# End of both mixers: half of the output projection held behind the last paged steps, and fewer, spread sums of squares in the attention's norm

## The chip, the cores and the metric

The kernel runs on one core of a Trainium2 chip. The metric is the device time of one execution in microseconds (us), as the median of several runs. The engines are named as the profile names them: PE (TensorE matmul), PEld (TensorE weight load), DVE (VectorE), ACT (ScalarE), POOL (GpSimd), SP (SyncE, which here only starts DMAs). TensorE's clock has two levels, 1.2 and 2.4 GHz; the profile gives the granted clock as a share of the higher one.

## The reference

One inference step of a decoder trunk with two layers, on 592 tokens together: 16 meta tokens and 512 prompt tokens of one sequence, and 8 sequences of 8 new tokens each. A layer is a half-step SwiGLU FFN, a mixer, and a second half-step FFN, each behind an RMSNorm and each added to the stream `x`. The mixer:

```python
z, xbc, dt_raw, q, k, v = split(h @ lp['w_in'])
y_ssd = ...                      # conv, SSD scan, gate, grouped RMSNorm: 512 columns
o = sb_block(q, ..., k_all, v_all, ...)   # stick-breaking attention, 8 heads x 64
y_sb = rms_norm(o.reshape(b, L, SB_WIDTH), lp['sb_out_norm'])
out = jnp.concatenate([y_ssd, y_sb], axis=-1) @ lp['w_out']
x = x + out
```

The prompt attends to itself. Each of the 8 sample sequences attends to 2048 old tokens, whose keys and values lie in pages of a cache, and to its own 8 new ones. The norm of `y_sb` needs for each token the sum of squares of all 512 attention outputs.

## The kernel before, in words

The stream lies in eight tiles `x` of 128 channels by 592 tokens. Every large product is made of three float32r products of split operands (high x high, high x low, low x high): `mm3` (L597) issues them for two halves of the tokens, 296 columns each (288 in the second mixer), so a weight block of 512 x 128 costs 24 matmuls at L602. `gemm` (L630) takes two such blocks per call: it loads the raw weights by SP (L584), splits them on ACT (L593) and DVE (L594), runs `mm3`, and then calls a function `done` on the PSUM result.

The program is written in one order, and the tile framework's planner then fixes, before the launch, the order of the instructions on each engine; an engine runs its instructions in that fixed order. The planner takes, of the instructions that its own clock holds ready, the one with the lowest number. `ahead` (L617) gives numbers inside the mixer, from the tables `PRI` and `UNIT` (L96, L97). Of those that meet here, in order: `wo0` 0, `wo3` 86, `wo6` 529, `pw7` 619, `tail` 799, `pv7` 1019, `ps7` 1031, `wo4` 1087, `wo7` 1477, `wo5` 1599, `wo2` 1775, `wo1` 2358. The program is traced once; the numbers are the same in both kernels.

The paged attention (`past`, L1444) goes through the 8 sample sequences. For each, `past_scores` (`ps`) gathers the keys by indirect DMAs of POOL (L1473, buffers `kn`, 6 of them), transposes them on DVE into `kt` (L1479, 2 buffers), multiplies (`sc`, recorded at L208 and L211) and takes two sigmoids. `past_weights` (`pw`) does the running products, a carry over 4 segments (L1504 to L1512), and 8 transposes on PE (L1520) that ACT copies to `wt`. `past_values` (`pv`, L1527) gathers values into 8 tiles `v`, from the same 6 buffers `kn`, and multiplies them by `wt` into `po` in four groups; then a mask (`ob`, L1550), a small product (L1554) and a copy (L1555) put 8 columns into `oP`, which after the eighth sequence has all 64.

`w_out` has 1024 rows. Its first 512 belong to the SSD half, and their product (L772, MH and ML, units `wo0` to `wo7` of 24 matmuls, 192 in all) needs nothing of the attention; `odone` adds it to `x` (L769). Behind these gemms in the program, the sample part is finished: `oP` times `tn` plus `on` (L774, L775, whole), and copies into the attention tiles `OT` (shown as `q`, L777, L778). `mix_sb` (L1258) makes the split operands `mh`, `ml` of `OT` (L1267, L1268) and the squares `gsq` (L1271), four tiles each, and calls `factor` (L553). `factor` starts a flow: one step of it is taken at each matmul of `mm3` (`step`, L607). Its first number is how many steps it waits, its third how many between the sums and the spread of the result; the second was read by nothing. It multiplies the squares by a column of ones to get one sum per token (`token_sums`, L472: five groups of 128 tokens times as many tiles as there are; each such matmul stands as two instructions at L476), takes 1/sqrt on DVE (L522 to L529, 14 small instructions with L566), and spreads it over the partitions with ten matmuls (L538) into `R` (L571). The second 512 rows of `w_out` (L793, again 192 matmuls) run meanwhile; their `last` (L784) needs `R`: it multiplies, adds to `x` (L789) and makes the operands of the next FFN and its sums of squares (`norm_tile`, L440, with an addition on POOL at L459).

## Time and profile before

| | |
|---|---|
| time, median of 3 runs | 2736.54 us (2730.8 to 2743.09) |
| the profiled execution: its own time | 2746.03 us |
| its span / mean granted clock | 2744.0 us / 0.975 |
| PE busy in it | 2641.0 us (96%) |
| DVE, ACT, POOL busy | 1502.8, 976.7, 313.4 us |
| HBM | 124 GB/s over the span |

The mixer of the first layer ends at about 962 us of the span, that of the second at about 2322. The FFNs lie before, between and behind. In the views a row of a stretch gives the busy time of each engine in it, the granted clock and the share of DMA; a row of the timeline gives start, duration, engine, line, operation, what it writes and reads, and in brackets how long its engine had been idle before it and what ended that.

### The profile page before, as it was taken

What the parts mean: (1) busy time and instruction counts of PE and PEld (TensorE: products, weight loads), DVE (VectorE), ACT (ScalarE), POOL (GpSimd) and SP (SyncE); (2) the same over time, 40 slices, a digit from 0 to 9 for tenths busy, and PEclk for the clock granted to TensorE, in tenths of its full rate; (3) what the DMA queues carried; (4) which work ended last, traced back from release to release, by engine and by line L of the source; (5) the groups of instructions that cost most, each with busy time, mean ns of one, the idle gap of its engine ahead of it and who ended that gap; (6) DMA issues with size and microseconds to landing.
All of it is one profiled execution on the core that took longest, in us unless ns stands there. A gap on an engine that the chain in (4) does not pass through costs nothing. (4 is left out here: it accounts for less than half of the span.)

```text
span 2744.0 us, 51377 instructions
## 1 busy us (share of the span) xinstructions
PE 2641.0 (96%) x21587; PEld 2497.2 (91%) x21587; DVE 1502.8 (55%) x2993; ACT 976.7 (36%) x1769; POOL 313.4 (11%) x288
## 2 busy tenths in 40 slices
PE   8999999999888899999999999999998899999999
PEld 7999999888657899999999999998876579999999
DVE  5444346477876544443554343455788856444444
ACT  3323224355663332222332222233556533322222
POOL 1000000023442100000000000000334421000000
PEclk9999999999998899999999999999999998999999
DMA  3232234357875122222222223243568751222222
GB/s 110 78 115 85 82 103 128 125 160 262 281 251 194 54 85 78 77 85 83 73 85 77 93 86 100 73 155 124 193 234 282 266 173 55 85 78 92 78 85 82
DMA packets 245110, 343.27 MB, mean 125 GB/s; under 512 B 32808, under 2 KB 196720, under 8 KB 244880
## 3 DMA queue, kind: packets, MB, share of 16 engines
q1 hardware_dynamic: 208016, 205.77, 23.7%
q0 software_dynamic: 36864, 134.23, 14.2%
q8 instruction: 169, 2.77, 0.4%
q14 instruction: 61, 0.50, 0.1%
HBM read 320.29 MB, written 19.66 MB: 124 GB/s over the span
## 5 line engine op out<-in xcount | busy, mean ns | idle before, releaser
L602 PE MATMUL g<-xl,whi 128*128 128x296 f32 (+1 forms) x3392 | 1018.7, 301 | 0.9 <-DVE xl L447 0.9
L602 PE MATMUL g<-xh,wlo 128*128 128x296 f32 (+1 forms) x3392 | 1013.5, 300 | 3.4 <-DVE wlo L594 3.4
L602 PE MATMUL g<-xh,whi 128*128 128x296 f32 (+1 forms) x3392 | 1014.9, 300 | 1.6 <-DVE gs L231 1.2
L593 ACT ACTIVATE whi<-raw 128x512 fp32r<-128x512 f32 (+1 forms) x664 | 412.8, 622 | 1373.7 <-PE g L602 1309.5
L594 DVE TENSOR_TENSOR wlo<-raw,whi 128x512 fp32r<-128x512 f32 (+1 forms) x664 | 450.7, 679 | 596.2 <-ACT whi L593 543.2
L602 PEld LDWEIGHTS g<-xh,wlo 128*128 128x128 f32 x3392 | 641.4, 189 | 5.8 <-DVE wlo L594 4.1
L602 PEld LDWEIGHTS g<-xh,whi 128*128 128x128 f32 x3392 | 640.4, 189 | 6.6 <-issue 3.0
L602 PEld LDWEIGHTS g<-xl,whi 128*128 128x128 f32 x3392 | 641.7, 189 | 4.0 <-issue 2.2
L602 PE MATMUL g<-hl,whi 128*128 128x296 f32 (+1 forms) x1408 | 417.8, 297 | 0.0
L602 PE MATMUL g<-hh,wlo 128*128 128x296 f32 (+1 forms) x1408 | 417.7, 298 | 0.0
L602 PE MATMUL g<-hh,whi 128*128 128x296 f32 (+1 forms) x1408 | 416.7, 298 | 0.0
L1473 POOL DMA_INDIRECT kn<-in_cache_k,ki x128 | 142.5, 1113 | 1546.7 <-PE g L602 931.4
L602 PEld LDWEIGHTS g<-hl,whi 128*128 128x128 f32 x1408 | 265.2, 188 | 0.0
L602 PEld LDWEIGHTS g<-hh,wlo 128*128 128x128 f32 x1408 | 264.4, 188 | 0.0
L602 PEld LDWEIGHTS g<-hh,whi 128*128 128x128 f32 x1408 | 263.9, 188 | 0.0
L1479 DVE STREAM_TRANSPOSE kt<-kn 128x512 f32<-128x512 f32 x256 | 163.6, 680 | 30.6 <-DMA kn<-in_cache_k,ki 17.2
L1537 POOL DMA_INDIRECT v<-in_cache_v,vi x128 | 137.2, 1072 | 336.0 <-PE po L211 175.2
L698 DVE SCALAR_TENSOR_TENSOR x<-g,x 128x296 f32<-128x296 f32 (+1 forms) x192 | 88.2, 464 | 118.9 <-PE g L602 118.4
L231 DVE TENSOR_TENSOR us<-g,R 128x296 f32<-128x296 f32 (+1 forms) x176 | 81.6, 464 | 130.5 <-PE g L602 130.4
L231 DVE TENSOR_TENSOR gs<-g,R 128x296 f32<-128x296 f32 (+1 forms) x176 | 80.7, 464 | 124.3 <-PE g L602 121.3
L602 PE MATMUL g<-mh,whi 128*128 128x296 f32 (+1 forms) x256 | 83.0, 332 | 4.8 <-ACT mh L1267 4.6
L602 PE MATMUL g<-ml,whi 128*128 128x296 f32 (+1 forms) x256 | 85.1, 333 | 0.0
(372 smaller groups left out, 2910.9 us busy)
## 6 DMA issues: line engine op xcount, KB each, us to landing
raw<-in_ffn_w_gu SPq DMA_DIRECT2D x176, 512.0 KB
raw<-in_ffn_w_down SPq DMA_DIRECT2D x80, 512.0 KB
raw<-in_w_in SPq DMA_DIRECT2D x44, 512.0 KB
raw<-in_w_out SPq DMA_DIRECT2D x16, 512.0 KB
spill<-x SPq DMA_DIRECT2D x16, 296.0 KB
x<-spill SPq DMA_DIRECT2D x16, 296.0 KB
raw<-in_ffn_w_down SPq DMA_DIRECT2D x16, 256.0 KB
xt<-in_x_prompt SPq DMA_DIRECT2D x8, 256.0 KB
```

What stands on the lines that cost most here:

```text
L231: self.nc.vector.tensor_tensor(tv[0:P, h, :], ps[h][0:P, 0:self.n], rv[0:P, h, :], ALU.mult)
L593: nc.scalar.activation(hi[:, 0:nk], s, AF.Copy)
L594: nc.vector.tensor_tensor(lo[:, 0:nk], s, hi[:, 0:nk].bitcast(F32), ALU.subtract)
L602: nc.tensor.matmul(ps[h][:, 0:self.n], w[:, k, :], self.hv(x)[:, h, :], start=(first and k == 0 and i == 0), stop=(last and k == nk - 1 an ...
L698: nc.vector.scalar_tensor_tensor(v, p, 0.5, v, ALU.mult, ALU.add)
L1473: nc.gpsimd.indirect_dma_start(kn, None, self.kflat, bass.IndirectOffsetOnAxis(ap=self.kidx[l][:, s, i:i + 1], axis=0))
L1479: nc.vector.transpose(kt[:, 2 * u:2 * u + 2].rearrange("p t h i -> p t (h i)"), kns[u][:, :, 256 * quad:256 * quad + 256])
L1537: nc.gpsimd.indirect_dma_start(v.rearrange("p k c -> p (k c)"), None, self.vflat, bass.IndirectOffsetOnAxis(ap=self.vidx[l][:, i, e:e + 1] ...
```

## The change

Three edits at the end of the mixer, and one in a helper.

1. Every matmul of the units `wo0` to `wo7` gets a dependency of order alone (no semaphore) on an instruction of the last paged steps: `wo0` to `wo3` on the last score matmul, `wo4` and `wo5` on the last transpose of the weights, `wo6` and `wo7` on the last value matmul. The planner may place them on PE only behind it.
2. The last two value tiles of the eighth sequence use the two buffers `kt` (the same 4096 bytes per partition) in place of `kn`.
3. `oP` is finished in two column ranges, 0 to 56 and 56 to 64, and its last addition writes into `OT` itself; the copies at L778 go.
4. `mix_sb` makes all of `mh` and `ml` first, then the squares, and adds them in pairs on DVE, so that two tiles go to `token_sums`. `factor` now waits 8 steps before the sums and takes two steps from sum to sum. The other two users of `factor` give 0 as the second number, which means one step as before.

```diff
             P = B[:, 0:5].unsqueeze(2)
-            yield from self.token_sums(P, squares, self.c_ones)
+            for _ in self.token_sums(P, squares, self.c_ones):
+                for _ in range(wait[1] or 1):
+                    yield
...
-    def mm3(self, ps, hi, lo, nk, XH, XL, first, last):
+    def mm3(self, ps, hi, lo, nk, XH, XL, first, last, after=None):
...
+                    if after:
+                        self.tc.add_manual_dep(mm, after.name, mybir.DependencyInfo(
+                            mybir.DependencyClass.NoSync, mybir.DependencyReason.DATA), reason="behind")
                     self.step()
...
         for mp in range(4):
-            self.gemm(wo, 0, 4, mp * 256, MH, ML, lambda m, ps: odone(2 * mp + m, ps))
-        nc.vector.tensor_tensor(self.oP, self.oP, self.tn, ALU.mult)
-        nc.vector.tensor_tensor(self.oP, self.oP, self.on, ALU.add)
+
+            self.gemm(wo, 0, 4, mp * 256, MH, ML, lambda m, ps: odone(2 * mp + m, ps),
+                      after=(self.last_sc, self.last_sc, self.last_pw, self.last_po)[mp])
         for m in range(4):
             nc.vector.tensor_copy(OT[m][:, 512:528], self.tail[:, m, :])
-            nc.vector.tensor_copy(OT[m][:, 528:592], self.oP[:, m, :])
+        for a, b in ((0, 56), (56, 64)):
+            o = self.oP[:, :, a:b]
+            nc.vector.tensor_tensor(o, o, self.tn[:, :, a:b], ALU.mult)
+            for m in range(4):
+                nc.vector.tensor_tensor(OT[m][:, 528 + a:528 + b], o[:, m, :], self.on[:, m, a:b], ALU.add)
...
+        for m, t in enumerate(OT):
             s = self.tmp("gsq")
             nc.scalar.activation(s[:, a:b], t[:, a:b], AF.Square)
-            sq.append(s)
-        self.factor(sq, 1.0 / 512, (0, 8, 20))
+            if m % 2:
+                nc.vector.tensor_tensor(sq[-1][:, a:b], sq[-1][:, a:b], s[:, a:b], ALU.add)
+            else:
+                sq.append(s)
+        self.factor(sq, 1.0 / 512, (8, 2, 20))
...
-                    v = self.kv.tile([128, 2, 512], F32, name="v", tag="kn", bufs=6)
+                    tag, bufs = ("kt", 2) if s == 7 and e + a2 == 2 else ("kn", 6)
+                    v = self.kv.tile([128, 2, 512], F32, name="v", tag=tag, bufs=bufs)
```

`self.last_sc`, `self.last_pw` and `self.last_po` are set to each score matmul, weight transpose and value matmul as it is issued, so that they hold the last of the layer; `gemm` hands `after` on to `mm3`.

## Rows read from the trace of the kernel before

**Rows 1.** The page's first part: busy time of each engine, its share of the span, and its instructions.
```profile
PE 2641.0 (96%) x21587; PEld 2497.2 (91%) x21587; DVE 1502.8 (55%) x2993; ACT 976.7 (36%) x1769; POOL 313.4 (11%) x288
```

**Rows 2.** Stretches of 5 us around the end of the first mixer. Columns: the stretch, its length, busy us (and instructions) of PE, PEld, DVE, ACT, POOL, granted clock, DMA share, GB/s.
```profile
835.00:840.00 5.00, 4.53 (x52) 3.68 (x52) 5.00 (x13) 3.03 (x5) 1.66 (x2) 0.50 0.36 107
855.00:860.00 5.00, 5.00 (x46) 4.21 (x45) 1.90 (x4) 2.21 (x5) 0.00 (x0) 1.00 0.32 105
900.00:905.00 5.00, 0.41 (x11) 0.34 (x12) 0.00 (x0) 0.00 (x0) 0.61 (x1) 0.99 0.61 210
920.00:925.00 5.00, 5.00 (x23) 5.00 (x24) 1.08 (x7) 0.28 (x1) 0.00 (x0) 0.50 0.00 0
```

**Rows 3.** The instructions of L602 alone in four stretches, two of each mixer: the stretch, its length, PE's busy us (count), PEld's, the granted clock, DMA share, GB/s.
```profile
849.50:865.30 15.80, 13.66 (x91) 12.60 (x91) 1.00 0.29 97
910.00:931.00 21.00, 17.53 (x64) 14.45 (x64) 0.63 0.09 26
2210.00:2218.60 8.60, 3.44 (x22) 2.99 (x22) 1.00 0.67 207
2267.00:2291.00 24.00, 18.08 (x65) 14.78 (x66) 0.58 0.07 23
```

**Rows 4.** What PE waited for in 840 to 915 us, and what POOL waited for in 840 to 905: the engine, line and tile that waited, for what, us in total, times, the longest.
```profile
PE po L208 <- DMA v<-in_cache_v,vi: 4.6, 1, 4.6
PE g L602 <- ACT mh L1267: 2.3, 1, 2.3
POOL v L1537 <- PE po L211: 41.3, 5, 22.1
```

**Rows 5.** The same for PE in 2205 to 2270 us.
```profile
PE g L602 <- ACT mh L1267: 2.4, 1, 2.4
```

**Rows 6.** The timeline of all engines at the end of the first mixer's paged part.
```profile
898.16 1.20 POOL L1537 DMA_INDIRECT v<-in_cache_v,vi  x1 [16.20 <-PE po L211]
904.61 0.38 PE L208 MATMUL po<-v,wt 128*32 128x256 f32 x1 [4.59 <-DMA v<-in_cache_v,vi]
906.32 0.42 DVE L1550 TENSOR_TENSOR ob<-po,call 128x256 f32<-128x256 f32 x1 [7.77 <-PE po L211]
906.79 1.04 PE L1554 MATMUL po<-call,ob 128*128 128x16 f32 x4 [0.52 <-DVE ob L1550]
907.87 0.19 DVE L1555 COPY oP<-po 128x32 f32<-128x32 f32 x1 [1.13 <-PE po L1554]
909.24 0.79 ACT L1267 ACTIVATE mh<-q,par 128x592 fp32r<-128x592 f32 x1 [11.42 <-DVE q L778]
910.08 1.85 PE L602 MATMUL g<-mh,whi 128*128 128x296 f32 x6 [2.25 <-ACT mh L1267]
```

**Rows 7.** The timeline of PE in the first mixer: the second weight transpose of the seventh sequence, and the last score block.
```profile
861.59 0.63 PE L1520 MATMUL pw<-call,pbe 128*128 128x128 f32 x4
870.69 0.35 PE L208 MATMUL sc<-kt,qbd 128*32 128x128 f32 x1
```

**Rows 8.** The timeline of DVE in the same stretch: key transposes, the weights that those transposes of PE read, and the last key transposes.
```profile
841.87 1.28 DVE L1479 STREAM_TRANSPOSE kt<-kn 128x512 f32<-128x512 f32 x2
846.55 0.73 DVE L1516 SCALAR_TENSOR_TENSOR pbe<-pbe,cq,pst 128x511 f32<-128x511 f32 x1
866.01 2.49 DVE L1479 STREAM_TRANSPOSE kt<-kn 128x512 f32<-128x512 f32 x4 [1.64 <-PE sc L211]
```

**Rows 9.** L476 alone in two stretches: the FFN norm's sums, and the attention's sums of the second mixer. Columns as in rows 3.
```profile
960.00:965.00 5.00, 2.34 (x20) 2.44 (x20) 1.00 0.36 111
2269.00:2285.00 16.00, 8.44 (x40) 10.29 (x40) 0.50 0.01 1
```

**Rows 10.** PE's timeline at either clock: the first and the last of 6 matmuls of L602 in a row, then of 12 in a row, then sums that stand in turn with single matmuls of L602, two at the higher clock and two at the lower.
```profile
889.80 0.45 PE L602 MATMUL g<-mh,whi 128*128 128x296 f32 x1
891.03 0.42 PE L602 MATMUL g<-mh,wlo 128*128 128x296 f32 x1
891.42 0.30 PE L602 MATMUL g<-ml,whi 128*128 128x296 f32 x1
892.95 0.30 PE L602 MATMUL g<-mh,whi 128*128 128x296 f32 x1
...
917.53 0.28 PE L476 MATMUL pw<-call,gsq 128*128 128x1 f32 x2
917.89 0.28 PE L476 MATMUL pw<-call,gsq 128*128 128x1 f32 x2
921.24 0.42 PE L476 MATMUL pw<-call,gsq 128*128 128x1 f32 x2
921.91 0.42 PE L476 MATMUL pw<-call,gsq 128*128 128x1 f32 x2
```

**Rows 11.** DVE's timeline from the moment that R stands in the first mixer: the multiplication by R, the addition to x without and with POOL's addition beside it, and the last operand of the next FFN.
```profile
932.03 0.84 DVE L231 TENSOR_TENSOR ot<-g,R 128x296 f32<-128x296 f32 x2 [1.57 <-ACT R L571]
932.90 0.77 DVE L789 TENSOR_TENSOR x<-x,ot 128x592 f32<-128x592 f32 x1
946.93 2.04 DVE L789 TENSOR_TENSOR x<-x,ot 128x592 f32<-128x592 f32 x1
961.35 0.83 DVE L447 SCALAR_TENSOR_TENSOR xl<-x,par,xh 128x592 fp32r<-128x592 f32 x1 [0.26 <-ACT xh L446]
```

More of the change, by code (lines that the diff above doesn't have):

```diff
@@ L601, in mm3 @@
                 for i, (w, x) in enumerate(((hi, XH[k]), (hi, XL[k]), (lo, XH[k]))):
-                    nc.tensor.matmul(ps[h][:, 0:self.n], w[:, k, :], self.hv(x)[:, h, :],
-                                     start=(first and k == 0 and i == 0),
-                                     stop=(last and k == nk - 1 and i == 2))
+                    mm = nc.tensor.matmul(ps[h][:, 0:self.n], w[:, k, :], self.hv(x)[:, h, :],
+                                          start=(first and k == 0 and i == 0),
+                                          stop=(last and k == nk - 1 and i == 2)).ins
+                    if after:
+                        self.tc.add_manual_dep(mm, after.name, mybir.DependencyInfo(
+                            mybir.DependencyClass.NoSync, mybir.DependencyReason.DATA), reason="behind")
                     self.step()
@@ L628, in ahead, with gemm @@
         return nullcontext() if d is None else self.tc.high_priority(max(0, now - d))
-    def gemm(self, src, r0, nk, c0, XH, XL, done, wide=2):
+    def gemm(self, src, r0, nk, c0, XH, XL, done, wide=2, after=None):
         kcs = []
@@ L650, in part @@
                 self.split0 = None
-            self.mm3(ps, hi, lo, n, XH[k:], XL[k:], k == 0, k + n == nk)
+            self.mm3(ps, hi, lo, n, XH[k:], XL[k:], k == 0, k + n == nk, after)
         wait = self.wait_done
@@ L1485, in past_scores @@
                         hd = 4 * (2 * (h % 2) + dh) + h // 2
-                        self.mm(sc[32 * i:32 * i + 32, quad, 128 * tb:128 * tb + 128],
+                        self.last_sc = self.mm(sc[32 * i:32 * i + 32, quad, 128 * tb:128 * tb + 128],
                                 qbd[:, hd].rearrange("p a q -> p (a q)"), kts[quad][:, :, 2 * i + dh, :],
@@ L1519, in past_weights @@
             for cc in range(4):
-                nc.tensor.transpose(pw[:, cc, :], be[quad][:, cc:512:4], self.ident)
+                self.last_pw = nc.tensor.transpose(pw[:, cc, :], be[quad][:, cc:512:4], self.ident).ins
             wt = self.kv.tile([128, 4, 16, 8], F32, name="wt", tag="wt")
@@ L1544, in past_values @@
                                 cc, g = 2 * e + j, 2 * j + quad
-                                self.mm(po[32 * g:32 * g + 32, 0:256],
+                                self.last_po = self.mm(po[32 * g:32 * g + 32, 0:256],
                                         wts[quad][:, a, 4 * cc:4 * cc + 4].rearrange("p h q -> p (h q)"),
```

## The prediction

> **What bounds the kernel now.** First the busy shares [rows 1]: PE is busy 2641.0 of 2744.0 us, the next engine 55%. So the time changes only where PE has less to do, waits less, or runs at a higher clock. Next the stretches around the end of a mixer [rows 2], which show both kinds of loss: in 900 to 905 us PE is busy 0.41 us of 5, and in 920 to 925 it is busy all the time at a granted clock of 0.50, the lower level of 1.2 GHz. What that level costs is in the pitch of the large matmuls [rows 10]: 5 steps from 889.80 to 891.03 are 0.246 us each, 11 steps from 891.42 to 892.95 are 0.139. The sums of squares stand in turn with single matmuls: 0.36 us per turn at the higher clock, so 0.36 - 0.139 = 0.22 for a sum (its two instructions), and 0.67 - 0.246 = 0.42 at the lower.
>
> Then the waits. In the first mixer PE waits 4.6 us for values and 2.3 for `mh` [rows 4], in the second 2.4 for `mh` [rows 5]. The timeline tells how that comes [rows 6]: POOL had stood 16.20 us before it could start the gather at 898.16, because its buffer was freed by the value matmuls themselves; the values let PE go on at 904.61; and from there mask, small product, copies and `mh` take until 910.08, 5.47 us with next to nothing on PE.
>
> Last, why the paged steps are late. The weights that PE transposes at 861.59 [rows 7] stand on DVE since 846.55 + 0.73 = 847.28 [rows 8]; keys were transposed by 841.87 + 1.28 = 843.15, and the last key transposes, at 866.01, name the score matmuls as what they waited for. Meanwhile, in 855 to 860, PE is full and DVE busy 1.90 of 5 us [rows 2], and between 849.5 and 865.3 PE runs 91 matmuls of `wo` [rows 3]. So the paged steps stand in PE's fixed order behind dense work that is ready early and has the lowest numbers, and when they are through, no dense work is left to cover their tail.
>
> **The change, part by part.**
>
> *Order.* The dependency is one of order alone, so no engine gets an instruction or a semaphore wait. What goes are the waits at the end: 4.59 + 0.52 + 2.25 = 7.36 us [rows 6] in the first mixer and 2.4 in the second, 9.8 together. The cover for the tail of 5.47 us is `wo6` and `wo7`, 48 x 0.139 = 6.7 us; without it the 9.8 come back. What is given up is the dense work in front of the last scores: 91 and 22 matmuls [rows 3], 12.6 and 3.1 us of PE. If the paged steps move forward into that place it costs nothing; if they don't, 15.7. Rows 7 and 8 are nearest and speak for the first, but between two score blocks lie 2.49 us of key transposes [rows 8], in which PE has only small work. I take 3 us for the first mixer and 1 for the second, +4. SP's loads of `w_out` move with the splits that free their buffers, by at most the 15.8 us of that stretch, and so does their use. In PE's queue the 48 held matmuls stand before the second half of the product, whose first operand needs the same tail, so they delay nothing while they are shorter than about the tail and `mh`: 5.47 us against 6.7, at most 1.2 per mixer, inside the +4.
>
> *Value buffers.* The last two gathers needn't wait for value matmuls; they follow the others on POOL, and nothing is queued behind them there that is needed before `norm_tile`. That is the 4.59, counted already. If it were the only thing that works, it would still give most of those 4.59 and nothing in the second mixer.
>
> *`oP`.* The last range is one multiplication and four additions on DVE, each no more than the 0.19 us of the copy at 907.87 [rows 6], where from that copy's end to `mh` it now takes 909.24 - 908.06 = 1.18. The first addition is enough for the first `mh`, so up to 0.8 us is gained; `wo7` hides it. Counted at 0; bare it would be -0.8 per mixer. The early range may be tied to the last copy too, five more small operations, +1.0; it is hidden in the same way.
>
> *Sums.* Ten sums per mixer go. From the first matmul of the second half until `R` stands, PE has 64 and 65 large matmuls [rows 3], 20 sums and 10 spreads, in 931.0 - 910.08 = 20.9 us and about 23.4 us, at granted clocks of 0.63 and 0.58. At the higher clock the same with ten sums is 64 x 0.139 + 10 x 0.22 + 10 x 0.139 = 12.5 us, and 12.6. That is -8.4 and -10.8, -19.2 if the clock stays high, and 2 x 10 x 0.42 = -8.4 if it stays low all the way. Which? The FFN norm has ten sums, in a block, and runs through them at 1.00; the attention's twenty in the second mixer run at 0.50 [rows 9]. Ten spread sums are nearer to the first row. I take four fifths, -15.4, since the planner may still put sums together and a part may begin cold.
>
> *What follows from `R`.* From 932.03 to 961.35 + 0.83 = 962.18 DVE works off the eight tiles behind `R` [rows 11], 30.2 us, partly at 2.04 us for an addition that takes 0.77 alone. PE reaches the next FFN with this chain close behind, so its gain counts only if `R` comes as much earlier. It does: `R` stood 22.0 us behind the first matmul of the second half; by the new numbers (8 + 20 + 20 + 10 = 58 steps of 0.139, 10 sums, 10 spreads of 0.139) it stands at 8.1 + 2.2 + 1.4 = 11.7, 10.3 earlier. The two additions of squares, 0.77 each by the same rows, come before the sums; they lie under `wo7` and the 8 steps, else +1.5 per mixer.
>
> Sum: -9.8 + 4 - 15.4 = -21.2 us. The profiled execution took 2746.03 us, so it would become 2724.8. It lies 9.5 above the median of the runs, so the median goes from 2736.5 to 2715.
>
> **Rivals.**
>
> *A cold front.* Where the dense matmuls are taken away the clock may fall. In 835 to 840 us PE is busy 4.53 us of 5 with paged and prompt steps, at 0.50 [rows 2]. Against it: in 2210 to 2218.6 PE spends only 3.44 of 8.6 us on large matmuls and the clock is 1.00 [rows 3]. Price: of the 23 us from 849.5 to the end of the last scores about 10.4 are other work than `wo`, of 2210 to 2219.6 about 6.5; at the lower clock each us becomes 0.246 / 0.139 = 1.77, so +8.0 and +5.0, of which some is hidden: +11 on the forecast, 2726. The Trainium skill, TensorE: Matmul & The Clock Gate, Part 4, says that transposes on PE don't count as activity for the clock in the way of other matmuls, and the paged steps are full of them; by that rule the whole +13 comes, 2728. The row of 835 to 840 agrees with it, the row of 2210 does not.
>
> *The sums still cost the clock.* The first operands and the squares share ACT, a `mh` takes 0.79 us [rows 6], so the squares are late, and the planner may issue the ten sums in one block; PE was busy all through 920 to 925 and still at 0.50. Then the second half keeps its low clock and only the instructions go: -9.8 + 4 - 8.4 = -14.2, 2722. Against it stands the FFN norm's block at 1.00 [rows 9].
>
> *The paged chain keeps its own time (slower).* If not PE's order but the chain of gathers, transposes, sigmoids and scans sets the last scores, they stay at 870.69 and the last values at 904.61. Then `wo6` and `wo7` come behind a cold wait: 48 x 0.246 = 11.8 us where 5.5 were, +6.3 in each mixer; the second half stays cold, -8.4, and its `R` comes later by 8 steps of 0.246 and two additions of 0.77, 3.5 us in each mixer, +7.0, with DVE's chain behind it. Together +11, and up to 3 us of cold `wo` more in the first: +13, 2749. It decides if the last scores end after about 870 us with the dense work behind them. Against it: rows 7 and 8, and POOL, which waited 41.3 us for value matmuls [rows 4].
>
> **How the numbers follow.** The forecast has 0.53 (2704 to 2724), the cold front 0.20, the cold sums 0.13, the slower chain 0.10; 0.04 is for better than 2704 (both mixers' 9.8 and 19.2 in full are 2707.5). A measurement of this kernel can tell about 0.5%, 13.7 us, from no change: below 2722.9 is faster, above 2750.2 slower. Faster: nine tenths of the forecast, a third of the cold front, half of the cold sums, and the 0.04, 0.65. Slower: half of the last rival and a remainder for an order by the planner that none of these foresees, 0.10. The range of 2696 to 2738 leaves out most of the last rival and that remainder.
>
> **What would show it.** Right: no matmul of `wo` before the last scores, and these near 855 us in place of 870.69; PE busy without a wait over 1 us from the last scores to the second half; the gathers of the last values issued without a stand of POOL for `po`; `wo6` and `wo7` on PE beside L1550 to `mh`; 40 instructions of L476 fewer on `gsq` (two mixers, ten sums, two each), a granted clock near 1.00 until `R`, and `R` about 12 us behind the first matmul of the second half. Wrong: PE idle or at 0.50 in front of the last scores for more than some 4 us; sums in one block with 0.50 behind it; or DVE's chain behind `R` leaving PE more than its present idle at the start of the second FFN.

## The result and the profile after

The changed kernel takes 2719.66 us (2713.74 to 2728.46), the kernel before in the same series 2738.68 (2730.80 to 2743.09). The medians lie 19.0 us apart; the ratio on record is 0.9942, with a 95% interval of 0.9928 to 0.9956, which is 15.9 us faster, between 12 and 20. The forecast was 21.5 us.

The two profiled executions differ by more, 2746.03 against 2716.29. The first lies 7.3 us above the median of its kernel, the second 3.4 below, so 10.7 of these 29.7 us are scatter. How large it is inside one part can be seen where all kernels have the same instructions in the same order: from the end of the first FFN to the last `zn` product of the first mixer it took 371.0 us in before, 370.4 in after, and 365.6 to 373.6 over the kernels below. So totals are taken from the timed runs, and places from the profiles. The profiled execution of the kernel e6 below is a slow one of 3909.85 us, whose granted clock falls to 0.16 at 2471 us, behind both mixers; only rows ahead of that are used.

PE is busy 29.1 us less, with 40 instructions fewer [rows 1]:

```profile
PE 2611.9 (96%) x21547; PEld 2469.2 (91%) x21547; DVE 1505.0 (55%) x3005; ACT 981.8 (36%) x1773; POOL 315.6 (12%) x288
```

The last scores of the first mixer, at 870.69 before [rows 7], and the first matmul of `wo`, at 849.58 before (L602 there, L605 now), in PE's timeline:

```profile
853.17 0.30 PE L208 MATMUL sc<-kt,qbd 128*32 128x128 f32 x1
853.31 0.94 PE L211 MATMUL sc<-kt,qbd 128*32 128x128 f32 x27
854.18 0.40 PE L605 MATMUL g<-mh,whi 128*128 128x296 f32 x1
```

The dense work now stands behind the paged steps, as the edit says. The end of those steps, in the timeline of all engines (what was [rows 6]):

```profile
885.68 1.11 PE L211 MATMUL po<-v,wt 128*32 128x256 f32 x11
886.71 0.40 PE L605 MATMUL g<-mh,whi 128*128 128x296 f32 x1
886.85 0.42 DVE L1565 TENSOR_TENSOR ob<-po,call 128x256 f32<-128x256 f32 x1 [3.78 <-PE po L211]
889.95 0.51 PE L1569 MATMUL po<-call,ob 128*128 128x16 f32 x4
```

The last values are multiplied at 885.68 and dense work follows at once; the small product (L1554 before) goes in between and makes PE wait for nothing. PE's waits in 845 to 930 us and in 2205 to 2280, and POOL's in 840 to 905 (what was [rows 4, 5]):

```profile
PE po L208 <- DMA v<-in_cache_v,vi: 1.0, 1, 1.0
PE g L605 <- DVE ot L231: 0.7, 1, 0.7
...
POOL v L1552 <- PE po L211: 9.1, 3, 8.4
...
PE g L605 <- DVE ot L231: 1.2, 1, 1.2
PE po L208 <- DMA v<-in_cache_v,vi: 0.7, 1, 0.7
```

Of the 4.6 for values 1.0 is left; the 0.5 for the mask and the 2.3 and 2.4 for `mh` are gone. POOL waits 9.1 us for value matmuls where it waited 41.3. A new wait, `g <- ot`, is short: a PSUM bank that is free only when `R` stands. Then the second half, L605 alone in 21 us from its first matmul in each mixer (against the second and fourth of [rows 3]), and L476 alone around the sums (against the second of [rows 9]):

```profile
899.30:920.30 21.00, 19.35 (x124) 17.19 (x124) 1.00 0.25 76
2249.10:2270.00 20.90, 18.78 (x126) 16.75 (x125) 1.00 0.25 77
...
899.00:906.00 7.00, 2.76 (x20) 3.23 (x20) 1.00 0.24 75
2247.00:2256.00 9.00, 2.77 (x20) 3.20 (x20) 1.00 0.21 61
```

124 and 126 large matmuls in 21 us, where there were 64 in 21 and 65 in 24, at a granted clock of 1.00 in place of 0.63 and 0.58, and 20 instructions of the sums where there were 40. DVE behind `R` [rows 11]:

```profile
912.76 0.84 DVE L231 TENSOR_TENSOR ot<-g,R 128x296 f32<-128x296 f32 x2 [3.37 <-ACT R L573]
927.65 2.04 DVE L799 TENSOR_TENSOR x<-x,ot 128x592 f32<-128x592 f32 x1
942.08 0.83 DVE L447 SCALAR_TENSOR_TENSOR xl<-x,par,xh 128x592 fp32r<-128x592 f32 x1 [0.26 <-ACT xh L446]
```

`R` stands 912.76 - 899.33 = 13.4 us behind the first matmul of the second half (22.0 before), and DVE's chain behind it takes 942.91 - 912.76 = 30.2 us, as before. It moved as a whole; the FFNs and the rest between the mixers take 875.0 us in both kernels.

For the sections that follow each mixer is cut in two. The *front* of the first mixer goes from the last `zn` product to the first matmul of the second half of the product, that of the second mixer from the end of the FFN ahead of it; the *half* goes from there to the last matmul of the product. The rows are a stretch, its length, busy us (and instructions) of PE, PEld, DVE, ACT, POOL, granted clock, DMA share, GB/s. Before:

```profile
832.90:910.08 77.18, 65.83 (x662) 54.88 (x661) 41.48 (x100) 25.08 (x52) 16.59 (x16) 0.88 0.46 154
910.08:949.18 39.10, 39.10 (x242) 38.79 (x242) 23.54 (x44) 14.91 (x25) 5.20 (x3) 0.80 0.13 41
1824.20:2267.65 443.45, 402.66 (x4110) 333.75 (x4109) 307.99 (x722) 215.67 (x451) 133.35 (x121) 0.95 0.61 206
2267.65:2308.61 40.96, 40.80 (x243) 40.26 (x243) 23.42 (x45) 15.05 (x25) 5.07 (x3) 0.76 0.13 40
```

After:

```profile
830.68:899.33 68.65, 63.31 (x664) 52.73 (x664) 44.04 (x107) 28.42 (x58) 17.13 (x16) 0.92 0.49 166
899.33:929.90 30.57, 29.82 (x223) 29.34 (x221) 21.84 (x43) 11.09 (x19) 5.85 (x3) 1.00 0.23 69
1804.90:2249.11 444.21, 404.36 (x4113) 334.89 (x4112) 310.64 (x729) 225.25 (x460) 137.22 (x121) 0.94 0.61 204
2249.11:2279.27 30.16, 28.94 (x224) 28.73 (x223) 22.23 (x45) 11.78 (x20) 5.14 (x3) 1.00 0.24 71
```

The first front is 8.5 us shorter, and both halves are (8.5 and 10.8). The second front, which holds the same end as the first, gained nothing. Its instructions also stand in another order than before, on DVE and ACT from about 1950 us on, 300 us ahead of the end that was edited.

The clock ahead of the last scores differs between the mixers. The rows are the first mixer of after up to its last scores, and then the 30 us up to the last score matmul of the second mixer in before, in after, and in e4, which has no order edit (see below):

```profile
838.50:853.10 14.60, 11.51 (x158) 8.43 (x156) 9.51 (x26) 7.62 (x18) 3.61 (x5) 1.00 0.60 195
...
2189.33:2219.33 30.00, 23.51 (x291) 18.30 (x291) 23.84 (x56) 12.97 (x27) 11.69 (x11) 0.89 0.67 231
...
2176.50:2206.50 30.00, 26.46 (x305) 20.47 (x305) 22.90 (x55) 15.30 (x33) 11.88 (x10) 0.66 0.61 193
...
2164.18:2194.18 30.00, 20.81 (x244) 15.13 (x242) 23.04 (x53) 12.52 (x26) 13.16 (x12) 0.66 0.60 190
```

In the first mixer the paged steps keep 1.00 without dense work among them. In the second their clock is 0.66 where it was 0.89, with the order edit and without it.

### The profile page after: what moved, and what is told of

The parts are those of the page before. It is cut to its first block, busy times and chain, and to the rows that moved or that the text cites. A ratio compares the mean times of both kernels' runs of the same rounds, so it can differ in the third digit from the quotient of the medians.

```text
span 2714.5 us, 51301 instructions
## 1 busy us (share of the span) xinstructions
PE 2611.9 (96%) x21547; PEld 2469.2 (91%) x21547; DVE 1505.0 (55%) x3005; ACT 981.8 (36%) x1773; POOL 315.6 (12%) x288
## 4 chain that ended last, share of the span: by engine, by line
PE 60%; DVE 6%; DMA 3%; ACT 2%; issue 1%; POOL 0%; SPq 0%; DVEq 0%; ACTq 0%; POOLq 0%
PE g L605 53%; DVE kt L1493 2%; DMA v<-in_cache_v,vi 1%; PE v L926 1%; DMA kn<-in_cache_k,ki 1%; PE po L208 1%; PE po L211 1%; DVE st L1298 1%; DVE x L799 0%; PE pw L476 0%; PE z L211 0%; PE sc L211 0%; DVE pst L1298 0%; PE zt L1350 0%; PE pw L1534 0%
## 5 line engine op out<-in xcount | busy, mean ns | idle before, releaser
L605 PE MATMUL g<-xl,whi 128*128 128x296 f32 (+1 forms) x3392 | 1016.9, 300 | 1.7 <-DVE xl L447 1.7
L605 PE MATMUL g<-xh,wlo 128*128 128x296 f32 (+1 forms) x3392 | 1012.5, 299 | 3.4 <-DVE wlo L596 3.4
L605 PE MATMUL g<-xh,whi 128*128 128x296 f32 (+1 forms) x3392 | 1013.8, 300 | 1.6 <-DVE gs L231 1.2
L605 PEld LDWEIGHTS g<-xh,wlo 128*128 128x128 f32 x3392 | 640.2, 189 | 5.4 <-DVE wlo L596 4.1
L605 PEld LDWEIGHTS g<-xh,whi 128*128 128x128 f32 x3392 | 639.6, 189 | 6.0 <-issue 2.6
L605 PEld LDWEIGHTS g<-xl,whi 128*128 128x128 f32 x3392 | 640.6, 189 | 4.8 <-DVE xl L447 2.8
L605 PE MATMUL g<-hl,whi 128*128 128x296 f32 (+1 forms) x1408 | 417.9, 297 | 0.0
L605 PE MATMUL g<-hh,wlo 128*128 128x296 f32 (+1 forms) x1408 | 417.7, 298 | 0.0
L605 PE MATMUL g<-hh,whi 128*128 128x296 f32 (+1 forms) x1408 | 416.8, 298 | 0.0
L1487 POOL DMA_INDIRECT kn<-in_cache_k,ki x128 | 137.0, 1070 | 1554.6 <-PE g L605 931.5
L605 PEld LDWEIGHTS g<-hl,whi 128*128 128x128 f32 x1408 | 265.2, 188 | 0.0
L605 PEld LDWEIGHTS g<-hh,wlo 128*128 128x128 f32 x1408 | 264.3, 188 | 0.0
L605 PEld LDWEIGHTS g<-hh,whi 128*128 128x128 f32 x1408 | 263.9, 188 | 0.0
L1552 POOL DMA_INDIRECT v<-in_cache_v,vi x128 | 144.2, 1127 | 280.6 <-DVE kt L1493 128.0
L691 ACT ACTIVATE hh<-us 128x592 fp32r<-128x592 f32 (+1 forms) x88 | 61.2, 696 | 62.4 <-DVE us L689 62.4
L605 PE MATMUL g<-mh,whi 128*128 128x296 f32 (+1 forms) x256 | 78.0, 305 | 2.0 <-DVE ot L231 2.0
```

The costliest lines, as they stand in the source:

```text
L605: mm = nc.tensor.matmul(ps[h][:, 0:self.n], w[:, k, :], self.hv(x)[:, h, :], start=(first and k == 0 and i == 0), stop=(last and k == nk - ...
L691: nc.scalar.activation(hh[:, a:b], u[:, a:b], AF.Copy)
L1487: nc.gpsimd.indirect_dma_start(kn, None, self.kflat, bass.IndirectOffsetOnAxis(ap=self.kidx[l][:, s, i:i + 1], axis=0))
L1552: nc.gpsimd.indirect_dma_start(v.rearrange("p k c -> p (k c)"), None, self.vflat, bass.IndirectOffsetOnAxis(ap=self.vidx[l][:, i, e:e + 1] ...
```

## The experiments

Each kernel is a version of before or after. The table collects all twelve, with before and after; fronts and halves are lengths in us of one profiled execution, ratios are to the kernel before, from the timed runs, with their 95% intervals. "O" is the order, "B" the value buffers together with the `oP` edit, "S" the sums.

| kernel | first front, half | second front, half | ratio |
|---|---|---|---|
| before | 77.2, 39.1 | 443.5, 41.0 | |
| O (e1) | 72.8, 37.9 | 454.3, 41.1 | 1.0012 (0.9999 to 1.0024) |
| S (e2) | 77.4, 33.6 | 461.7, 32.6 | 1.0029 (1.0017 to 1.0041) |
| B (e11) | 69.4, 36.9 | 443.2, 37.4 | 0.9994 (0.9979 to 1.0009) |
| O B (e3) | 70.8, 36.9 | 447.3, 34.0 | 0.9998 (0.9984 to 1.0012) |
| O S and `oP` (e5) | 68.2, 29.7 | 458.2, 32.8 | 0.9950 (0.9934 to 0.9966) |
| B S (e4) | 70.7, 31.4 | 435.8, 29.4 | 0.9923 (0.9904 to 0.9943) |
| B S again (e12) | 70.7, 32.7 | 435.7, 29.4 | 0.9920 (0.9904 to 0.9936) |
| after (O B S) | 68.7, 30.6 | 444.2, 30.2 | 0.9942 (0.9928 to 0.9956) |
| after, twenty sums, spread (e6) | 69.9, 33.1 | 456.1, 32.0 | 0.9978 (0.9963 to 0.9992) |
| after, ten sums, not spread (e7) | 68.5, 29.6 | 453.3, 28.7 | 0.9937 (0.9917 to 0.9957) |
| O B S in the first mixer (e8) | 70.7, 30.6 | 454.3, 37.5 | 0.9990 (0.9973 to 1.0007) |
| O B S in the second mixer (e9) | 77.5, 39.0 | 438.8, 31.3 | 0.9965 (0.9949 to 0.9981) |
| B S, O in the second mixer (e10) | 69.4, 31.5 | 443.4, 29.4 | 0.9925 (0.9906 to 0.9944) |

### One edit alone, and after without one

**Order alone (e1_order).** Before, with the dependency and nothing else:

```diff
-            self.gemm(wo, 0, 4, mp * 256, MH, ML, lambda m, ps: odone(2 * mp + m, ps))
+            self.gemm(wo, 0, 4, mp * 256, MH, ML, lambda m, ps: odone(2 * mp + m, ps),
+                      after=(self.last_sc, self.last_sc, self.last_pw, self.last_po)[mp])
```

> The kernel before with the order of the output product alone (its last three pairs behind the last score, the last pw transpose and the last value matmul); twenty sums, old buffers, old oP. The stretch from the last zn product to the last matmul of the output product is 116.3 and 112.5 us in before, 99.2 and 96.9 after. Theory (order covers the waits, the sums keep the clock): only the waits go, less the value buffers' 4.59 where they still bind; 107 to 112 and 107 to 111, ratio to before 0.996 to 0.999, the granted clock behind the twenty sums still 0.50 for some 10 us or more. Rival (the gap alone let the clock fall): with the gap closed the twenty sums run at 1.00, 103 to 105 in each, ratio about 0.993. Rival (slower chain): no gain, ratio 1.000 or above.

Measured: 110.7 us in the first mixer, inside the theory's range, and no gain in all, 1.0012, which it doesn't allow. The rival of the slower chain has this ratio, but not by its mechanism: the last scores begin at 854.3 us where the last began at 872.1, and PE waits for nothing from 875 to 915. The first mixer's half at a clock of 0.86:

```profile
903.04:940.95 37.91, 36.83 (x246) 36.69 (x245) 24.65 (x47) 14.44 (x24) 5.24 (x4) 0.86 0.17 53
```

The second mixer took back what the first gave: its front is 454.3 us where it was 443.5. There the stretch from `zn` that the expectation uses is no measure any more (87.6 us), since `zn` itself has another place in the new order; therefore the second front is counted from the end of the FFN.

**Sums alone (e2_sums).** Before, with this and the second number of `factor` read as in after:

```diff
+        for m, t in enumerate(OT):
             s = self.tmp("gsq")
             nc.scalar.activation(s[:, a:b], t[:, a:b], AF.Square)
-            sq.append(s)
-        self.factor(sq, 1.0 / 512, (0, 8, 20))
+            if m % 2:
+                nc.vector.tensor_tensor(sq[-1][:, a:b], sq[-1][:, a:b], s[:, a:b], ALU.add)
+            else:
+                sq.append(s)
+        self.factor(sq, 1.0 / 512, (8, 2, 20))
```

> The kernel before with halved and spread sums alone; old order, buffers and oP. Theory (gain of the sums is their instructions plus the clock of the second half, 8.4 and 10.8 at most): 106 to 109 and 102 to 105 us for the stretch of 116.3 and 112.5, ratio 0.993 to 0.996, R some 12 us behind the first matmul of the second half. Rival (the gap in front lets the clock fall, whatever the sums do): only the instructions at the low clock, 4.2 each, 112 and 108, ratio 0.997, granted clock 0.50 for some 10 us behind the gap.

Measured: 111.0 in the first mixer, between theory and rival, and 1.0029, slower than either allows. The second number, 111.4, is counted from a `zn` that has moved (as in e1). The half of the first mixer loses 5.5 us, not the full 8.5, because it begins at a low clock behind the waits that are still there. The rows are the waits, the whole half, and its first 5.5 us:

```profile
PE po L208 <- DMA v<-in_cache_v,vi: 4.5, 1, 4.5
PE g L605 <- ACT mh L1275: 2.3, 1, 2.3
...
910.57:944.16 33.59, 32.51 (x224) 32.37 (x225) 25.67 (x48) 15.77 (x26) 5.24 (x4) 0.92 0.16 48
910.57:916.10 5.53, 5.53 (x23) 5.53 (x24) 4.60 (x6) 4.33 (x7) 0.00 (x0) 0.50 0.00 0
```

So the rival was partly right: the gap in front costs clock too. The second half of the second mixer gained 8.4 us; its front came out 18.2 us longer, with the last scores behind most of the dense work, ending at 2253.0 us.

**Order and buffers, old sums (e3_no_sums).** After, with `token_sums` and `mix_sb` of before.

> The kernel after with the old twenty sums, one per matmul: order, value buffers and oP alone. Theory: the waits go (7.4 and 2.4, less some 1 to 4 of new idle time), the second half stays at a low clock for 10 to 20 us: 107 to 112 and 108 to 111 us for the stretch, ratio 0.996 to 0.998. Rival (the gap let the clock fall): 103 to 105, ratio 0.993, a granted clock of 1.00 through the twenty sums.

Measured: 107.6 and 102.1; 0.9998. The first mixer is in the theory's range, the ratio is above it. The second number is again counted from a `zn` that has moved. PE waits for nothing from 860 to 921 us, so it comes to the twenty sums without a gap, and they still run at a lower clock. The rows are L476 alone, the half, and two stretches of all instructions, PE busy all through both:

```profile
897.00:911.50 14.50, 6.69 (x40) 8.52 (x40) 0.78 0.11 36
...
901.23:938.09 36.86, 36.65 (x242) 36.16 (x240) 21.84 (x43) 11.32 (x19) 5.67 (x3) 0.86 0.19 58
...
896.00:905.00 9.00, 9.00 (x72) 9.00 (x71) 5.98 (x10) 3.83 (x7) 0.00 (x0) 1.00 0.18 58
905.20:915.40 10.20, 10.20 (x46) 10.20 (x45) 2.84 (x15) 0.63 (x1) 0.00 (x0) 0.50 0.09 26
```

The clock fell while the sums ran, with PE busy. That ends the rival by which the gap alone let the clock fall. In the second mixer the half came to 34.0 us, at 0.90.

**Without the order (e4_no_order, e12_no_order).** After, with the call of `gemm` of before.

> The kernel after without the order of the output product: value buffers, oP, halved and spread sums alone. Theory: last score again near 870; the 4.59 us for values goes where the gathers can start earlier, the 2.25 for mh stays; with the gain of the sums 102 to 105 us in the first mixer and 102 to 105 in the second, ratio 0.993 to 0.996. Rival (order is what moves the values and the buffers add nothing): as the sums alone, 106 to 109 and 102 to 105. Rival (order is nothing): as after, 99 and 97, ratio 0.993.

Measured: 102.1 in the first mixer, as the theory says, and 0.9923. The last scores begin at 866.3 us, late as expected. Without the order only 0.5 and 1.5 us of wait remain at the end of the first front (e4), and the half is at 1.00:

```profile
PE g L605 <- ACT mh L1276: 1.5, 1, 1.5
...
PE po L1568 <- DVE ob L1564: 0.5, 1, 0.5
...
898.23:929.66 31.43, 30.21 (x224) 29.96 (x225) 25.68 (x48) 15.78 (x26) 5.24 (x4) 1.00 0.17 51
```

The second mixer, 435.8 + 29.4, is the shortest so far, and the ratio is below the theory's range. The kernel was measured a second time beside the one with the order in the second mixer alone:

> The same kernel as the one after without the order of the output product, which came out at 0.9923 from few runs, beside the one with the order in the second mixer alone. Theory (it is better than after): 0.991 to 0.9935, first mixer 470 to 473, second 464 to 467. Rival (it is as after, and the first result was a chance): 0.994 to 0.996.

0.9920, second mixer again 435.7 + 29.4, both as the theory says. The first mixer's 474.6, against 470 to 473, is not; it has a half of 32.7 us at a granted clock of 0.95.

**Old buffers (e5_no_buffers).** After, with

```diff
-                    tag, bufs = ("kt", 2) if s == 7 and e + a2 == 2 else ("kn", 6)
-                    v = self.kv.tile([128, 2, 512], F32, name="v", tag=tag, bufs=bufs)
+                    v = self.kv.tile([128, 2, 512], F32, name="v", tag="kn", bufs=6)
```

> The kernel after with the old value buffers (all in kn); order, oP and sums as in after. From the end of the first FFN to the end of the mixer: 487.3 us in before, 469.6 in after for the first mixer, 484.4 and 474.4 for the second. Theory (the order takes the last values away from the end, so the buffers are worth at most the 3.1 us that lie between the first mixer with order alone, 110.7, and with order, buffers and oP, 107.6): first mixer 470 to 473. Rival (the buffers are the main gain: with the sums they gave 8.9 in the first mixer, 111.0 against 102.1): 476 to 479. The total depends on how the planner orders the second mixer, which has come out between 465 and 495 in the runs so far: no number for it.

Measured: first mixer 468.4, even below the theory's range and no longer than in after; the rival falls. With the order there, the buffers are worth nothing that shows in the first mixer. The second front is 458.2, and the ratio 0.9950.

**Buffers and `oP` alone (e11_buffers_only).** After, without order and with the old sums.

> The kernel before with the value buffers and oP alone; old order, old sums. Theory: in the first mixer the 4.59 us for the last values goes, the waits for mh and the small product stay, and the twenty sums in a row keep their low clock: 487.3 to 481 to 484. Rival (the idle time in front is what lets the clock fall): with most of it gone the second half runs at 1.00, 471 to 476. Second mixer: order as in before until its last 100 us, 480 to 485. Ratio 0.996 to 0.999 by the theory, 0.993 to 0.996 by the rival.

Measured: 473.3 in the first mixer. That is the rival's number by another way: the half still runs at 0.86, and the gain is in the front, 7.8 us, more than the 4.6 us of the wait. The second mixer is in another order than before from about 1950 us on, and not only in its last 100 us.

```profile
825.46:894.89 69.43, 62.77 (x662) 52.44 (x662) 41.42 (x104) 25.18 (x52) 17.24 (x16) 0.93 0.50 171
894.89:931.82 36.93, 36.93 (x242) 36.52 (x242) 23.56 (x44) 14.91 (x25) 5.19 (x3) 0.86 0.15 44
```

PE's busy time in the front fell by 3.1 us at the same 662 instructions, and the clock rose from 0.88 to 0.93. How much of this is the gap's is not shown: e4, e12 and e10 run the same front in the same order and have 70.7, 70.7 and 69.4 us, at 0.90, 0.90 and 0.93. The total, 0.9994, is that of neither theory nor rival, and less than this profile shows. This execution took 2724.0 us where the median of the runs is 2734.6, and where the others lose is not shown.

What follows from these seven: in the first mixer, order and buffers do the same thing. The length of the front also holds the clock's scatter, as after and e8 show, which have the same order there and take 68.7 and 70.7 us. PE's idle time in it (length less busy time) tells more: 11.0 to 13.3 us with neither (before, e2, e9), 5.2 and 5.8 with the order (e5, e1), 5.8 to 6.8 with the buffers and `oP` (e4, e12, e11, e10), and 4.8 to 5.3 with all three (after, e3, e6, e7, e8). Either closes the gap, and both together close little more. The sums give 5.5 us in the half behind a gap; where the gap is closed they give 4.3 and 5.5 (B to B S), 6.3 (O B to after) and 8.2 (O to O S).

### What holds the clock: fewer sums, or spread sums

**Spread, not halved (e6_spread_only).** After, with all four tiles of squares:

```diff
-            if m % 2:
-                nc.vector.tensor_tensor(sq[-1][:, a:b], sq[-1][:, a:b], s[:, a:b], ALU.add)
-            else:
-                sq.append(s)
+            sq.append(s)
```

> The kernel after with all twenty sums (squares not added in pairs), still one per two matmuls. Theory A (spreading holds the clock): clock 1.00 through the second half of the first mixer, only the instructions of ten sums more, 10 x 0.22 = 2.2 us, and a later R with less cover: first mixer 472 to 474. Theory B (fewer one-column matmuls are what holds it): some 10 us at 0.50 in the second half, first mixer 475 to 478, as without the new sums (478.2).

**Halved, not spread (e7_halved_only).** After, with

```diff
-        self.factor(sq, 1.0 / 512, (8, 2, 20))
+        self.factor(sq, 1.0 / 512, (0, 1, 20))
```

> The kernel after with the sums halved but not spread: ten sums from the first step on, one per matmul, as the twenty stood in before. In the first mixer, from the end of the first FFN to the end of the mixer, 469.6 us in after, 472.3 with twenty sums spread, 478.2 with twenty in a row. Theory (spreading is what holds the clock, halving saves only the instructions): some 7 to 10 us at 0.50 in the second half, first mixer 473 to 477. Rival (halving holds it as well): no low clock in the second half, R earlier by some 18 steps, first mixer 467 to 470.

Measured: 472.3 and 466.2, by theory A for e6 and just below the rival's range for e7. The first mixer's halves, e6 and then e7:

```profile
899.89:932.95 33.06, 31.98 (x244) 31.84 (x243) 22.60 (x45) 12.05 (x20) 5.21 (x4) 1.00 0.21 65
```

```profile
895.06:924.65 29.59, 29.59 (x225) 29.59 (x224) 23.06 (x45) 11.66 (x19) 8.51 (x4) 1.00 0.23 72
```

Both are at 1.00, against 0.86 with twenty in a row. So either part holds the clock alone, and the theory that only spreading does has fallen. Both kernels also make all operands before the squares, which e3 doesn't. That wasn't tried alone; as PE waits for nothing in e3's sums, it could act only through where the sums stand among PE's matmuls, which is what both parts change. The halving is worth more: 36.9 to 29.6 alone, where spreading alone gives 36.9 to 33.1. On top of the halving the spreading costs 1.0 and 1.5 us (29.6 to 30.6, 28.7 to 30.2): `R` comes later, and PE waits for a PSUM bank, 0.7 and 1.2 us (`g <- ot`, above), where e7 has no wait in its halves. The same wait of 1.2 us stands in e9's second half just ahead of 2276 to 2279 us at 0.50. It depends on what lies around: e5's first half, spread too, has no wait and takes 29.7. In the timed runs e7 (0.9937) and after (0.9942) are the same.

### The second mixer's order

**The whole change in one mixer (e8_first_only, e9_second_only).** After, with a condition on the layer in all the edits, as in

```diff
-                      after=(self.last_sc, self.last_sc, self.last_pw, self.last_po)[mp])
+                      after=(self.last_sc, self.last_sc, self.last_pw, self.last_po)[mp] if l == 0 else None)
```

and with `l == 1` for the other.

> The whole change in the first mixer alone; the second mixer has the code of before. Theory (the planner orders the second mixer anew from whatever state the first leaves, so part of each total is an order that the change doesn't aim at): first mixer 469 to 471, second mixer off 484.4 by more than 3 us either way, its instructions on PE, DVE and ACT in another order than in before long before its end. Rival (the second mixer's part of the difference is the chip's own scatter): second mixer 484.4 to within 2 us and the same order, total 2726 to 2728 profiled, ratio 0.9935.

> The whole change in the second mixer alone; the first mixer has the code of before. Theory: first mixer 487 to 488; the second starts from the state of before, so its early part keeps the order and the times of before, and only its end gains, the 15.6 us by which its last stretch is shorter in after (112.5 to 96.9): second mixer 467 to 471, ratio 0.994 to 0.995. Rival (the middle of the second mixer is made slower by the change itself, not by another start): 474 as in after, ratio 0.996 to 0.997.

Measured: e8 491.8 us for the second mixer, whose code is that of before, and 0.9990; e9 470.1 and 0.9965. The second front, cut 125.8 and 200 us behind the end of the FFN, in before, e9 and e8:

```profile
1824.20:1950.00 125.80, 125.80 (x1007) 116.22 (x1006) 74.89 (x193) 47.39 (x97) 15.70 (x11) 1.00 0.44 140
1950.00:2150.00 200.00, 177.15 (x2019) 141.00 (x2019) 153.15 (x340) 117.71 (x249) 76.22 (x73) 0.95 0.70 236
2150.00:2267.65 117.65, 99.71 (x1087) 76.53 (x1087) 79.94 (x191) 50.57 (x108) 41.44 (x38) 0.91 0.64 225
```

```profile
1948.90:2148.90 200.00, 175.22 (x2023) 139.70 (x2021) 156.79 (x344) 121.11 (x256) 78.84 (x75) 0.97 0.73 243
2148.90:2261.90 113.00, 102.02 (x1089) 80.44 (x1090) 80.23 (x195) 51.25 (x106) 39.70 (x37) 0.86 0.62 219
```

```profile
1927.40:2127.40 200.00, 177.13 (x1944) 140.09 (x1942) 146.44 (x324) 120.43 (x243) 73.41 (x69) 0.91 0.69 226
2127.40:2255.87 128.47, 107.60 (x1163) 83.67 (x1162) 86.99 (x207) 53.78 (x117) 46.49 (x42) 0.88 0.65 221
```

In 200 us PE gets through 2019 instructions in before, 2023 in e9, and 1944 in e8, which is also after's number. In e9, DVE's and ACT's order in the second mixer is that of before up to about 2200 us; in e8 it is after's for the first 395 us of the mixer, and differs from before's from 1950 on. So the change in the first mixer alone makes the planner order the second one anew, although nothing was edited there.

That this order is worse follows from the timed runs. The end of e8's first mixer is 15.0 us shorter than before's (101.3 against 116.3), and the whole kernel only 2.7 us (7.4 less to 1.9 more), so some 8 to 17 us are lost behind it, where only the second mixer's order differs. The 10.8 us of e8's second front agree with that: 7.9 are busy time of PE, for as many instructions at a clock of 0.93 in place of 0.95, and 2.9 are idle time. One profile alone wouldn't settle it, because the front of one and the same order varies by 7.7 us (e10, below). The rival (the chip's own scatter, with the order of before) falls.

The first mixers, 466.9 in e8 and 489.7 in e9, miss their ranges by the scatter of their early parts (365.6 and 373.2 us). For e9 the profile is in the theory's range, 484.4 - 470.1 = 14.3 us, and the timed runs give the rival's number, 0.35% or 9.6 us; the profiled before lies 7.3 above its median, which is enough for the difference.

Seven other kernels were also ordered anew from 1950 on, with fronts of 443.2 to 461.7. Those without order in the first mixer but with buffers and sums (e4, e12, e10) keep before's order to about 2150. Why the first mixer's end changes the planner's choice there, and not in those three, was not tried and stays open.

**Order in the second mixer only (e10_order_second).** After, with `if l == 1 else None` behind the dependency alone.

> The kernel after with the order of the output product in the second mixer alone; buffers, oP and sums in both. Theory (in the first mixer the order is worth 2 to 3 us and costs 5 to 20 in the second, whose work the planner then orders anew from its start; in the second mixer it shortens the end and disturbs nothing): first mixer 470 to 473 as without the order, second mixer no longer than the 465.2 without the order, 460 to 466; ratio 0.990 to 0.992. Rival (the second mixer came out at 465.2 by luck of the plan, and any other plan comes out near its mean of 480): 475 to 485, ratio 0.995 to 0.997.

Measured: 471.6 in the first mixer, as expected; 472.8 in the second, between the two; 0.9925. But the edit changes nothing here. In e4 and e12 no matmul of `wo` stands ahead of the second mixer's last scores to begin with, and on PE, PEld, DVE, ACT and POOL the instructions of e10 stand in the order of e4 and e12 from the first to the last, but for one pair on PE that starts within 0.01 us. So the three are executions of one order, and the second fronts, e10 and then e12, show how far such executions differ:

```profile
1807.00:2250.38 443.38, 403.88 (x4111) 334.16 (x4110) 310.20 (x727) 218.81 (x455) 132.11 (x121) 0.95 0.60 205
```

```profile
1810.60:2246.27 435.67, 397.59 (x4112) 331.46 (x4110) 309.79 (x727) 218.71 (x455) 134.48 (x121) 0.96 0.62 208
```

They are 7.7 us apart: PE is busy 6.3 us less in e12 with the same work, and idle 1.4 less. Neither theory nor rival is decided, and what the order is worth in the second mixer is not shown by this run. After without the order gave 0.9923, 0.9920 and 0.9925. Each of the three intervals overlaps with that of after, so that it beats after is likely and not settled; it beats before by about 21 us.

## Why the prediction was right, and where it wasn't

The number was right: 2715 against 2719.66, inside the range, faster by more than 0.5%. By its steps:

- *What bounds the kernel.* Right. Both losses were real, and both went.
- *Order, -9.8 + 4.* In the first front 8.5 us went where -7.36 + 3 = -4.4 was forecast. The last scores moved to 853 us, and behind 845 us PE waits 1.0 us at most. Of the 8.5, 6.0 are idle time of PE, and 2.5 are busy time at a clock of 0.92 in place of 0.88. For the clock in the front the term had nothing, and it is partly scatter: e8, in the same order, is 2.1 us longer busy. But the step's reasoning failed in one place: "without it the 9.8 come back". Without the order (e4) 2.1 us of waits come back in the first mixer, and the front is 70.7 against after's 68.7 and e8's 70.7, which have it.
- *Value buffers, "the 4.59, counted already".* They were held to be a small part of the order's gain. Alone, with `oP`, they close nearly all of the first mixer's gap (e11, e4), and where the order is there they add nothing that shows (e5).
- *`oP` at 0.* It was not run by itself. Where no dense work hides it, in e4 and e11, the wait for `mh` is 1.53 us where it was 2.25, a gain of 0.7, and the forecast gave it 0.8 bare. In after it is hidden, as said.
- *Sums, -15.4.* The mechanism was right and the size low: the halves lost 8.5 and 10.8 us, the full 19.3, since the clock stays at 1.00 throughout. Not all of that is the sums' own: alone they gave 5.5 and 8.4 (e2), since behind a gap the half begins at 0.50. The forecast had no term for this tie between gap and sums. Four fifths were taken for fear of sums in one block; e7 shows that ten in a row hold the clock, too, as the FFN norm's block suggested [rows 9].
- *`R` at 11.7 us.* 13.4: PE's timeline has 70 large matmuls between the first of the second half and the spreads, 43 of them behind the last sum, where 58 were counted; the 12 more are 1.7 us. The bank wait of 0.75 us comes behind `R`. DVE's chain kept its 30.2 us and moved along, as said.
- *Rivals.* The cold front didn't come in the first mixer, where the steps up to the last scores run at 1.00 from 838.5 us on; the 0.50 ahead of that stands in before, too [rows 2]. In the second a cold stretch did: 0.66 in place of 0.89 in the last 30 us, which is one of the prediction's signs of being wrong. The order edit isn't its cause, as e4 has the same 0.66 without it. Nor is it enough that no dense work stands ahead, as e6 and e7 have none there and 0.89. What it cost is not shown apart from the new order. The Trainium skill (TensorE: Matmul & The Clock Gate, Part 4) says that transposes on PE don't count for the clock in the way of other matmuls, and by that it would have come in both mixers. The first doesn't bear it out: 8 transposes of L1534 (L1520 before) lie in the 14.6 us at 1.00. The second agrees with it. Sums that still cost the clock: not in after, but so with twenty in a row (e3). The slower chain: not by its mechanism, the scores moved as the forecast said.
- *What was missing.* The second mixer's front: forecast at -1.4, and by e9 worth -4.7, it came out at +0.8, and in e8, with no edit there, at +10.8. The prediction had "an order by the planner that none of these foresees" in a remainder of the slower side, and no term for it. By the timed runs of e8 the loss is real, though 10.8 is from one profile. This give-back is the likely reason why two terms that were larger than forecast ended in a gain smaller than forecast.

So the forecast's total came out near partly by luck: gains at the ends under-estimated by some 8 us (4.1 in the first front, 3.9 in the halves) stand against a loss in the second mixer's front that was not seen at all. How the rest of the profiled 29.7 us divides between these and the scatter of 10.7 can't be told from single executions.

## What to carry to other kernels

When a planner fixes the order, an edit is priced at its own place and then once more everywhere behind it: compare the order of unedited stages before crediting an edit, and try it in one stage at a time. Compare the order of the edited stage too: where it is the same, a difference in time is scatter, however well it fits a theory. Two edits that close the same gap are worth about one. One-column matmuls in a long row cost more than their own time here, because the clock of the dense work around them fell with them; halving them was worth more than spreading them, and spreading delays their result.

## What the runs showed of the hardware that was not expected

PE's clock fell to 0.50 without any wait in front of it (e3, 905.2 to 915.4 us), and was held at 1.00 with the same sums in other places (e6). The forty sum instructions of the first mixer took 6.69 us of PE in a row (granted clock 0.78 over their stretch, e3) and the same forty 5.55 us when spread at two matmuls each, at 1.00 (e6), L476 alone:

```profile
896.00:911.50 15.50, 5.55 (x40) 6.48 (x40) 1.00 0.22 69
```

The other surprise is how much the clock moves one fixed order. Three executions of the same instructions in the same order have second fronts of 435.8, 435.7 and 443.4 us (e4, e12, e10), of which 6.3 us are busy time of PE at 0.96 and 0.95. PE's idle time in them, 38.0, 38.1 and 39.5 us, repeats better than the length here.
